# A recurrence's operands loaded in the fifth and sixth step of its chain, and a square placed between two transposes

## The chip, the cores and the metric

One NeuronCore of a Trainium2 chip. The time is that of one execution on the device, in microseconds; of several runs the median counts. Engines are called as in the profile: PE is TensorE, DVE VectorE, ACT ScalarE, POOL GpSimd, and SP is SyncE, which in this kernel only issues DMAs.

## The reference

Two layers of an encoder for 512 tokens of width 1024: layer 0 mixes tokens by windowed attention, layer 1 by a recurrence in both directions (RWKV-7), and a convolutional feed-forward part follows each. The change concerns the recurrence alone. Cut to what matters:

```python
def wkv7_scan(r, w, k, v, a, bb, reverse):          # per head, state 64 x 64
    def step(state, inp):
        r_t, w_t, k_t, v_t, a_t, b_t = inp
        sa = jnp.einsum('bhvk,bhk->bhv', state, a_t)
        state = state * w_t[:, :, None, :] + sa[..., None] * b_t[:, :, None, :] + v_t[..., None] * k_t[:, :, None, :]
        y = jnp.einsum('bhvk,bhk->bhv', state, r_t)
        return state, y
...
    y = y_f + y_b                                    # forward and backward scan, 16 heads
    mean = jnp.mean(y, axis=-1, keepdims=True)
    var = jnp.mean(jnp.square(y - mean), axis=-1, keepdims=True)
    yn = ((y - mean) * lax.rsqrt(var + RWKV_GN_EPS)).reshape(b, s, d) * lnx_w.astype(F32) + lnx_b.astype(F32)
    out = (yn + (bonus_f + bonus_b).reshape(b, s, d)) * g.astype(F32)
    return out.astype(h.dtype) @ w_o
```

## The kernel before

The 16 heads are handled as eight column tiles of two heads each (`ct`, 0 to 7); the 512 tokens of a tile are eight chunks of 64, in both directions `d`. For each tile the projections (`rwkv_proj`) make four scaled operands and store them to HBM: `ar` holds [a | r], `bk` holds [b | k], each 1 MB for a tile with both directions. `rwkv_scan` then works on a tile in stages:

- `prep` loads `bk` and `ar` of a tile. There are two buffers for `bk` and three for `ar`, so a load waits for the last reader of an older tile.
- `low` multiplies `ar` with `bk` on PE; DVE masks the products into `bw` (line 943). `blocks` stores the diagonal blocks to HBM (`ls`), `loaded` reads them back in another layout as `X`.
- `solve` inverts these triangular blocks in 31 small steps, three on POOL, seventeen on DVE, the rest on POOL (lines 1005 and 1007). DVE copies the result (line 913, `X<-Y`), `kept` stores it (`zs`), `inverses` reads it back as `t32` (`t` in the trace) and `tt`, and `level` makes the full inverses of it.
- `tokens` transposes `bk` on PE, ACT copies the result into `bw` (line 911). `sides` transposes `a` and multiplies with `v` (lines 981 and 983).
- `batch` combines all into the chain's matrices; `step` is one step of the chain: products with the state on PE, and the scaling to the next state on ACT (line 1124, `st`), in seven of the eight steps.
- `head_norm` normalizes a finished tile in five parts (`n0` to `n4`); part `n1` squares on ACT (line 1147), and the last stores the tile (`os`).

`run` goes through the tiles in iterations `i` from -1 to 7. An iteration walks through the eight strings of `K.between`, one per step; `c` is the chain's step for tile `i`, and the other letters are parts for the same or a later or earlier tile: `m1` and `n` finish tile `i` and tile `i - 1`, `t`, `a`, `L`, `x0`, `x1`, `m0`, `z`, `I` belong to tile `i + 1`, `l`, `b`, `X` and the solving steps `G`, `V` to tile `i + 2`, and `p` loads tile `i + 3`. `e` loads `gt` and `bo`, which `n4` needs.

All instructions from the start of `run` on are tied to the order in which they are written, engine by engine; the DMAs too, since SP issues them all. What is ahead of `run` (projections, `low` of tiles 0 and 1, the first inverse) is ordered by the compiler's scheduler.

Of the kernel before, what the change touches and what calls it, by code (L numbers as in the profile page):

```python
# [52 lines left out]
def paced(K, later, earlier):  # L53

    K.tc.add_manual_dep(later.ins, earlier.ins.name,
                        mybir.DependencyInfo(mybir.DependencyClass.Sync, mybir.DependencyReason.DATA), reason="pace")
# [766 lines left out]
def rwkv_scan(K, A, sc, mid):  # L823

    nc = K.nc
# [5 lines left out]
    R = Ctx()  # L831
# [22 lines left out]
    def mk(shape, name, bufs=1, dt=F32):  # L854
        pool = mid if name in MID else pools[next((k for k, v in PLACE.items() if name in v), "batch")]
        return pool.tile(shape, dt, name=name, tag=name, bufs=bufs)
# [17 lines left out]
    def spare(n):  # L874
        pool = R.pre.enter_context(tc.tile_pool(name=f"pre{len(R.pres)}", bufs=1, space=PSUM, side="right", reuse_waits="tile"))
        R.pres += [pool.tile([P, S], F32, name=f"pre{i}") for i in range(n)]
# [7 lines left out]
    def start():  # L884

        pools["early"] = first.enter_context(tc.tile_pool(name="early", bufs=1, side="right", reuse_waits="tile"))
        spare(K.npre)
        R.ARs, R.BKs, R.BWs = [], [], []
        inputs(1)
        R.Xs, R.nX = [mk([P, 32, 32], "X0")], 0  # L890
        R.cs = []
        R.done = dict.fromkeys("pls", 0)

    R.start = start

    def inputs(n, bks=True):

        for _ in range(n):
            R.ARs.append(mk([P, 2, 2, NC, HD], f"ar{len(R.ARs)}"))
            if bks:  # L900
                R.BKs.append(mk([P, 2, NC, 2, HD], f"bk{len(R.BKs)}"))
            R.BWs.append(mk([P, 2, NC, 2, 3 * HD], f"bw{len(R.BWs)}").rearrange("p d c e s -> p c d e s"))
# [16 lines left out]
    def prep(ct):  # L919

        c = Ctx()
        ar, bk = R.ARs[ct % len(R.ARs)], R.BKs[ct % len(R.BKs)]
        c.AR, c.BK = [ar[:, d] for d in range(2)], [bk[:, d] for d in range(2)]
        nc.sync.dma_start(out=bk, in_=sc["bk"][ct].rearrange("d p c z s -> p d c z s"))
        nc.sync.dma_start(out=ar, in_=sc["ar"][ct].rearrange("d p z c s -> p d z c s"))
        return c

    def bk(c, d, e, q):

# [2 lines left out]
    def low(ct, c, g):  # L932


        c.BW = R.BWs[ct % len(R.BWs)]
        hf, d = GROUPS[g]
        pvs = [bank().rearrange("p (c s) -> p c s", c=4) for _ in range(2)]
        for i in range(4):
            q = 4 * hf + i
            for e in range(2):  # L940
                T.matmul(pvs[e][:, i], lhsT=bk(c, d, e, q), rhs=c.AR[d][er(e), :, at(d, q)], start=True, stop=True)
        for e in range(2):
            V.tensor_tensor(out=c.BW[:, 4 * hf:4 * hf + 4, d, e, 0:P], in0=pvs[e],
                            in1=R.mask[:, d, None, :].broadcast_to([P, 4, P]), op=ALU.mult)

    def blocks(ct, c, d):

        for h in range(2):
            nc.sync.dma_start(out=sc["l"][ct, h, d].rearrange("c e i j -> i c e j"),
                              in_=c.BW[qr(d, h), :, d, :, 32 * h:32 * h + 32])  # L950

    def loaded(ct, c):
        c.X = block()
        for b in range(2):
            nc.sync.dma_start(out=c.X[er(b)], in_=sc["l"][ct].rearrange("h d c e i j -> (h d c e) i j"))
# [59 lines left out]
    def kept(ct, c):  # L1015
        zd = sc["z"][ct]
        for d in range(2):
            nc.sync.dma_start(out=zd[0, 48 * d:48 * d + 16], in_=c.Z[0][HD + 48 * d:HD + 48 * d + 16])
        nc.sync.dma_start(out=zd[1], in_=c.Z[1][0:HD])

    def go(ct, c, n, by):

        c.by = by
        if not hasattr(c, "solving"):
            c.solving = solve(ct, c)
        for _ in range(n):
            next(c.solving, None)
# [152 lines left out]
    def stages(names):  # L1180

        for x in names:
            ct = R.done[x]
            R.done[x] += 1
            K.ct = ct
            if x == "p":
                R.cs.append(prep(ct))
            elif x == "l":
                for g in range(4):
                    low(ct, R.cs[ct], g)  # L1190
                for d in range(2):
                    blocks(ct, R.cs[ct], d)
                loaded(ct, R.cs[ct])
            else:
                go(ct, R.cs[ct], 32, "G")
                kept(ct, R.cs[ct])
# [5 lines left out]
    def part(i, q):  # L1202

        x, args = q[0], [int(k) for k in q[1:].split(",") if k]
        if x == "p":
            while len(R.cs) <= min(i + 3, KT - 1):
                K.ct = len(R.cs)
                R.cs.append(prep(K.ct))
            return
        if x in "xm":  # L1210
            k, fn, args = i + (q != "m1"), batch, [args[0], int(x == "m")]
        else:
            k, fn = i + PARTS[x][0], PARTS[x][1]
            if x in "GVgv":
                fn, args = go, args + [x.upper()]
        if 0 <= k < KT and not (x == "z" and k == 0) and not (x in "lbX" and k < R.done["l"]):
            K.ct = k
            fn(k, R.cs[k], *args)

    def run(last):  # L1220
# [13 lines left out]
        for i in range(-1, KT):  # L1234
            more = None
            if i == KT - 1:
                first.close()
                more = last(R)
            for j in range(NC):
                K.ct = max(i, 0)  # L1240
                for q in K.between[j].split():
                    if q == "c":
                        K.ct = i
                        if i >= 0:
                            step(i, R.cs[i], j)
                    else:
                        part(i, q)
                if more and j:
                    next(more, None)
# [24 lines left out]
def body(ctx, tc, A, out, stage=9):  # L1274
    nc = tc.nc
    K = Ctx()
# [47 lines left out]
    K.begin, K.tail = (2,), ("pl", "", "", "")  # L1324
    K.ny = 2
    K.eng.update(z0="V", z1="V")
    K.between = ("w0 c l0 l1 b0 u g4", "c l2 l3 b1 g4 z X I", "c m1 w1 n0 e", "c n1 t0 t1 G3", "c a0 n2 V6", "c L0 n3 V6", "c L1 a1 n4 p V5", "c x0 x1 m0 G4")
    const = ctx.enter_context(tc.tile_pool(name="const", bufs=1, reuse_waits="tile"))

    @contextmanager  # L1330
# [54 lines left out]
    def ffn(layer, xT, st, nxt, nst, store):  # L1385
# [4 lines left out]
    sc = {"ar": dram.tile([KT, 2, P, 2, NC, HD], F32, name="ars"), "bk": dram.tile([KT, 2, P, NC, 2, HD], F32, name="bks"),  # L1390
          "v": dram.tile([S, D], F32, name="vs"), "g": dram.tile([KT, P, S], F32, name="gs"),
          "bo": dram.tile([KT, P, S], F32, name="bos"), "o": dram.tile([KT, P, S], F32, name="os"),
          "l": dram.tile([KT, 2, 2, NC, 2, 32, 32], F32, name="ls"), "z": dram.tile([KT, 2, HD, 32, 32], F32, name="zs")}
# [14 lines left out]
    if stage <= 1:  # L1408
        for e in (xstack, products, left, banks):
            e.close()  # L1410
        return
    scan = rwkv_scan(K, A, sc, mid)
    scan.late, scan.pre = left, banks
    rwkv_proj(K, xT, st, xstack, products, A, sc, scan)

    with ExitStack() as end:
# [64 lines left out]
        with tc.tile_pool(name="act2", bufs=1, reuse_waits="tile") as K.act:  # L1481
            K.accp = K.work = K.act
            on_tile = residual(xT, "nch1" if stage > 2 else None, st if stage > 2 else None, out if stage == 2 else None)
            for ot in range(KT):
                ps = scan.bank()
                c = slice(ot * P, (ot + 1) * P)
# [84 lines left out]
```

## Time and profile before

| | |
|---|---|
| runs | 1612.32, 1612.32, 1610.83 us; median 1612.32 |
| profiled execution | 1611.12 us, of which the span from first to last instruction is 1608.9 |
| PE busy | 1481.5 us (92%) |
| DVE, ACT, POOL busy | 1033.6 (64%), 689.9 (43%), 441.8 (27%) |
| chain that ended last, by engine | PE 67%, DVE 14%, DMA 7%, POOL 5%, issue 4% |
| loads of `ar`, of `bk` | 8 each, 1024 KB, median 8.5 and 5.2 us from issue to landing |

The busy shares are means over the whole program, and the stages differ: the feed-forward layers fill PE, the scan (about 929 to 1173 us of the span) does not. The chain that ended last is followed back from the last instruction; a DMA in it means that an engine waited for this transfer.

### The profile page before, as it was taken

What the parts mean: (1) busy time and instruction counts of PE and PEld (TensorE: products, weight loads), DVE (VectorE), ACT (ScalarE), POOL (GpSimd) and SP (SyncE); (2) the same over time, 40 slices, a digit from 0 to 9 for tenths busy, and PEclk for the clock granted to TensorE, in tenths of its full rate; (3) what the DMA queues carried; (4) which work ended last, traced back from release to release, by engine and by line L of the source; (5) the groups of instructions that cost most, each with busy time, mean ns of one, the idle gap of its engine ahead of it and who ended that gap; (6) DMA issues with size and microseconds to landing.
All of it is one profiled execution on the core that took longest, in us unless ns stands there. A gap on an engine that the chain in (4) does not pass through costs nothing.

```text
span 1608.9 us, 28508 instructions
## 1 busy us (share of the span) xinstructions
PE 1481.5 (92%) x11612; PEld 1198.3 (74%) x11612; DVE 1033.6 (64%) x1643; ACT 689.9 (43%) x1228; POOL 441.8 (27%) x533
## 2 busy tenths in 40 slices
PE   8989999999999998989987588777889999999999
PEld 7767688888888886767765477666767888888887
DVE  6876457777773348968988656665547677777222
ACT  5576534444432224556543343333444444444111
POOL 2630003222310015425488423223200333221000
PEclk9999999999999999999996597888899999999999
DMA  5200022333233332446536545555343222323331
GB/s 187 79 27 1 11 95 92 99 98 99 97 99 112 101 95 66 131 154 216 188 140 200 167 107 140 135 134 142 82 161 130 92 92 92 101 96 102 103 120 56
DMA packets 108834, 178.56 MB, mean 111 GB/s; under 512 B 49184, under 2 KB 62112, under 8 KB 108704
## 3 DMA queue, kind: packets, MB, share of 16 engines
q1 hardware_dynamic: 108560, 176.75, 36.2%
q8 instruction: 91, 1.49, 0.4%
q14 instruction: 39, 0.32, 0.1%
q10 hardware_dynamic: 144, 0.00, 0.0%
HBM read 142.64 MB, written 34.08 MB: 110 GB/s over the span
## 4 chain that ended last, share of the span: by engine, by line
PE 67%; DVE 14%; DMA 7%; POOL 5%; issue 4%; ACT 2%; SPq 1%; DVEq 0%; POOLq 0%; ACTq 0%
PE mm L113 17%; PE mm L111 16%; PE mm L112 16%; DMA ar<-ars 2%; PE mm L394 2%; PE sc L111 2%; PE sc L112 2%; PE sc L113 2%; DMA X<-ls 2%; POOL Y L1007 2%; PE tp L389 2%; DVE wlo L78 1%; POOL tg L1005 1%; DVE tv L1005 1%; DMA ls<-bw 1%
## 5 line engine op out<-in xcount | busy, mean ns | idle before, releaser
L75 ACT CAST whi<-wraw 128x1024 fp32r<-128x1024 f32 (+1 forms) x197 | 201.0, 1022 | 258.2 <-PE mm L112 179.4
L111 PE MATMUL mm<-hl,whi 128*128 128x512 f32 x720 | 281.3, 391 | 2.0 <-DVE xT L1368 1.8
L113 PE MATMUL mm<-hl,wlo 128*128 128x512 f32 x720 | 281.7, 391 | 0.8 <-POOL wlo L78 0.4
L112 PE MATMUL mm<-hl,whi 128*128 128x512 f32 x720 | 281.0, 390 | 0.0
L78 DVE TENSOR_TENSOR wlo<-wraw,whi 128x1024 fp32r<-128x1024 f32 (+1 forms) x140 | 167.1, 1194 | 170.2 <-ACT whi L75 169.7
L78 POOL TENSOR_TENSOR wlo<-wraw,whi 128x1024 fp32r<-128x1024 f32 x57 | 136.7, 2398 | 400.6 <-ACT whi L75 386.8
L192 DVE SCALAR_TENSOR_TENSOR conv<-upad,par,conv 128x512 f32<-128x512 f32 x88 | 125.6, 1429 | 64.1 <-ACT conv L189 64.1
L113 PEld LDWEIGHTS mm<-hl,wlo 128*128 128x128 f32 x720 | 135.6, 188 | 32.4 <-POOL wlo L78 3.1
L111 PEld LDWEIGHTS mm<-hl,whi 128*128 128x128 f32 x720 | 135.5, 188 | 30.2 <-ACT hl L98 2.2
L112 PEld LDWEIGHTS mm<-hl,whi 128*128 128x128 f32 x720 | 135.6, 188 | 28.3
L113 PE MATMUL mm<-gh,wlo 128*128 128x512 f32 x352 | 139.0, 395 | 0.0
L111 PE MATMUL mm<-gh,whi 128*128 128x512 f32 x352 | 139.0, 395 | 0.0
L112 PE MATMUL mm<-gl,whi 128*128 128x512 f32 x352 | 139.0, 395 | 0.0
L104 ACT CAST gh<-gact 128x512 fp32r<-128x512 f32 x44 | 27.4, 623 | 140.4 <-DVE gact L201 140.4
L189 ACT ACTIVATE conv<-upad,par 128x512 f32<-128x512 f32 x88 | 71.7, 816 | 21.7 <-DVE upad L187 21.5
L113 PEld LDWEIGHTS mm<-gh,wlo 128*128 128x128 f32 x352 | 66.1, 188 | 16.1
L111 PEld LDWEIGHTS mm<-gh,whi 128*128 128x128 f32 x352 | 66.1, 188 | 16.1
L112 PEld LDWEIGHTS mm<-gl,whi 128*128 128x128 f32 x352 | 66.1, 188 | 16.0
L1005 POOL TENSOR_TENSOR tg<-X,Y 128x56 f32<-128x56 f32 (+16 forms) x129 | 46.3, 359 | 111.3 <-DVE Y L1007 81.3
L194 DVE SCALAR_TENSOR_TENSOR conv<-upad,par,conv 128x512 f32<-128x512 f32 x88 | 70.1, 798 | 3.0
L1124 ACT ACTIVATE st<-bank,gc 128x64 f32<-128x64 f32 x112 | 29.5, 318 | 91.4 <-PE bank L1121 87.5
L199 ACT ACTIVATE silu<-conv 128x512 f32<-128x512 f32 x44 | 27.9, 634 | 91.2 <-DVE conv L194 91.2
(334 smaller groups left out, 3148.4 us busy)
## 6 DMA issues: line engine op xcount, KB each, us to landing
wraw<-in_w_up_dram SPq DMA_DIRECT2D x88, 512.0 KB, 3.6
wraw<-in_w_down_dram SPq DMA_DIRECT2D x32, 512.0 KB, 3.6
ars<-tab SPq DMA_DIRECT2D x16, 512.0 KB, 2.7
bks<-tab SPq DMA_DIRECT2D x16, 512.0 KB, 3.4
ar<-ars SPq DMA_DIRECT2D x8, 1024.0 KB, 8.5
bk<-bks SPq DMA_DIRECT2D x8, 1024.0 KB, 5.2
wraw<-in_w_down_dram SPq DMA_DIRECT2D x16, 384.0 KB, 3.2
wraw<-in_w_qkv_dram SPq DMA_DIRECT2D x11, 512.0 KB, 4.3
```

The lines of the kernel that those rows point to most:

```text
L75: nc.scalar.copy(out=hi, in_=raw)
L78: lo_engine.tensor_tensor(out=lo, in0=raw, in1=hi.bitcast(F32), op=ALU.subtract)
L111: nc.tensor.matmul(ps, lhsT=lhs[0], rhs=rhs[0], start=first, stop=False)
L112: nc.tensor.matmul(ps, lhsT=lhs[0], rhs=rhs[1], start=False, stop=False)
L113: nc.tensor.matmul(ps, lhsT=lhs[1], rhs=rhs[0], start=False, stop=last)
L189: nc.scalar.activation(out=c, in_=u[:, 1:S + 1], func=AF.Identity, scale=K.par[:, cw + 2 * FT + ch:cw + 2 * FT + ch + 1], bias=K.par[:, cb ...
L192: nc.vector.scalar_tensor_tensor(out=c, in0=u[:, 0:S], scalar=K.par[:, cw + ch:cw + ch + 1], in1=c, op0=ALU.mult, op1=ALU.add)
L194: nc.vector.scalar_tensor_tensor(out=c, in0=u[:, 2:S + 2], scalar=K.par[:, cw + 4 * FT + ch:cw + 4 * FT + ch + 1], in1=c, op0=ALU.mult, op ...
L389: nc.tensor.transpose(out=tp[:, j * P:(j + 1) * P], in_=p[:, e, j * P:(j + 1) * P], identity=K.ident)
L394: nc.tensor.matmul(po[e * HD:(e + 1) * HD, n], lhsT=vn[:, n - 1 + j, kv * HD:(kv + 1) * HD], rhs=pT[:, e, j * P:(j + 1) * P], start=n == 0 ...
L1005: en.tensor_tensor(out=tm, in0=X[:, 0:kx, kx:kx + 1].broadcast_to([P, kx, n]), in1=Y[:, kx:kx + 1, m:16].broadcast_to([P, kx, n]), op=ALU. ...
L1007: en.tensor_tensor(out=Y[:, 0:kx, m:16], in0=Y[:, 0:kx, m:16], in1=tm, op=ALU.add)
```

## The change

`prep` becomes a generator. It loads each direction of `bk` and of `ar` by a DMA of its own, 512 KB each, first `bk`, then `ar`. Once the chain runs (`R.pace` is then the last scaling on ACT), each load waits for that scaling, and `prep` stops after `bk`; the new letter `q` lets it go on with `ar`. `p` moves from the seventh string of `K.between` (behind `n4`) to the fifth, `q` stands in the sixth, and in the fourth `n1` moves from ahead of both transposes to between them.

```diff
         R.done = dict.fromkeys("pls", 0)
+        R.pace = R.prep = None
...
-        nc.sync.dma_start(out=bk, in_=sc["bk"][ct].rearrange("d p c z s -> p d c z s"))
-        nc.sync.dma_start(out=ar, in_=sc["ar"][ct].rearrange("d p z c s -> p d z c s"))
-        return c
+        for x, name in ((bk, "bk"), (ar, "ar")):
+            for d in range(2):
+                src = sc[name][ct, d]
+                ld = nc.sync.dma_start(out=x[:, d], in_=src)
+                if R.pace:
+                    paced(K, ld, R.pace)
+            if R.pace:
+                yield c
+        yield c
...
             if x == "p":
-                R.cs.append(prep(ct))
+                R.cs.append(next(prep(ct)))
...
         if x == "p":
             while len(R.cs) <= min(i + 3, KT - 1):
                 K.ct = len(R.cs)
-                R.cs.append(prep(K.ct))
+                R.prep = prep(K.ct)
+                R.cs.append(next(R.prep))
+            return
+        if x == "q":
+            if R.prep:
+                next(R.prep, None)
+                R.prep = None
             return
...
-    K.between = ("w0 c l0 l1 b0 u g4", "c l2 l3 b1 g4 z X I", "c m1 w1 n0 e", "c n1 t0 t1 G3", "c a0 n2 V6", "c L0 n3 V6", "c L1 a1 n4 p V5", "c x0 x1 m0 G4")
+    K.between = ("w0 c l0 l1 b0 u g4", "c l2 l3 b1 g4 z X I", "c m1 w1 n0 e", "c t0 n1 t1 G3", "c a0 p n2 V6", "c L0 q n3 V6", "c L1 a1 n4 V5", "c x0 x1 m0 G4")
```

On SP, the end of the third string to the start of the next iteration, before (`gt`, `bo`: operands of the last part of the norm; `os`: the store of a normalized tile; `ls`: the blocks for the next inverse):

```order
L1037 DMA tt0_7306<-zs_78 32x16x32 x4
L1062 DMA gt_8592<-gs_74 128x512
L1064 DMA bo_8594<-bos_75 128x512
L1166 DMA os_76<-t_8902 128x512
L924 DMA bk0_5951<-bks_72 128x2x1024
L925 DMA ar1_7303<-ars_71 128x2x1024
L949 DMA ls_77<-bw1_7305 32x16x32 x2
```

The loads of a later tile stand behind the store here. The same place on SP now:

```order
L1044 DMA tt0_7308<-zs_78 32x16x32 x4
L1069 DMA gt_8600<-gs_74 128x512
L1071 DMA bo_8602<-bos_75 128x512
L928 DMA bk0_5951<-bks_72 128x1024 x2
L928 DMA ar1_7305<-ars_71 128x1024 x2
L1173 DMA os_76<-t_8914 128x512
L956 DMA ls_77<-bw1_7307 32x16x32 x2
```

The loads have changed places with the store, and are four instead of two. In the first iteration of the chain there is no `gt`, `bo` or `os`, and the loads stand behind `tt` in both.

On ACT, the fourth step, before (`st`: the scaling; `t_8612`: the square; `bw`: the copies of the transposes, two for each direction):

```order
L1124 ACTIVATE st_8600<-bank_8546,gc_5023 128x64 x2
L1147 ACTIVATE t_8612<-t_8590 128x512
L911 COPY bw2_7483<-mm_7301 128x8x64
L911 COPY bw2_7483<-mm_7302 128x8x64
L911 COPY bw2_7483<-pre0_5948 128x8x64
L911 COPY bw2_7483<-pre1_5949 128x8x64
L1124 ACTIVATE st_8671<-bank_8607,gc_5023 128x64 x2
```

Here the square stands ahead of all four copies. The same step on ACT now:

```order
L1131 ACTIVATE st_8608<-bank_8554,gc_5023 128x64 x2
L912 COPY bw2_7487<-mm_7303 128x8x64
L912 COPY bw2_7487<-mm_7304 128x8x64
L1154 ACTIVATE t_8638<-t_8598 128x512
L912 COPY bw2_7487<-pre0_5948 128x8x64
L912 COPY bw2_7487<-pre1_5949 128x8x64
L1131 ACTIVATE st_8679<-bank_8615,gc_5023 128x64 x2
```

The square has moved behind the first direction's two copies; nothing else differs in this step.

On SP in the projections, where the scheduler places the first tile's loads (`ar_5950`, `bk_5951`) among the stores of a later tile's operands (`tab`), before and now:

```order
-L775 DMA ars<-tab 128x1024
-L779 DMA bks<-tab 128x1024
-L925 DMA ar_5950<-ars 128x2x1024
-L61 DMA wraw<-in_wk_dram 128x1024
-L924 DMA bk_5951<-bks 128x2x1024
...
+L928 DMA ar_5950<-ars 128x1024
+L775 DMA ars<-tab 128x1024
+L928 DMA bk_5951<-bks 128x1024
+L779 DMA bks<-tab 128x1024
```

The first half of each load has moved ahead of the stores; in what follows, `low` of tile 0 and the first solving steps stand a few instructions earlier on PE, DVE and POOL, and before the end of the projections one half of tile 2's `bk` stands on SP ahead of the last tile's loads and stores.

## Rows read from the trace of the kernel before

**Rows 1.** Busy time in two stretches: PE, PEld, DVE, ACT, POOL, granted clock, DMA.

```profile
1020.00:1080.00 60.00, 45.78 (x1089) 40.76 (x1089) 37.13 (x97) 20.66 (x60) 18.46 (x54) 0.83 0.48 127
...
972.00:984.00 12.00, 10.09 (x274) 9.10 (x274) 5.97 (x19) 5.38 (x14) 4.01 (x10) 0.57 0.64 146
```

**Rows 2.** Timeline of DVE, the copies of finished inverses: start, duration, [idle before].

```profile
935.62 2.10 DVE L913 COPY X<-Y 64x512 f32<-64x512 f32 x4
...
967.84 2.09 DVE L913 COPY X<-Y 64x512 f32<-64x512 f32 x4 [0.45 <-POOL Y L1007]
...
1004.03 2.08 DVE L913 COPY X<-Y 64x512 f32<-64x512 f32 x4
...
1079.99 2.09 DVE L913 COPY X<-Y 64x512 f32<-64x512 f32 x4
...
1118.34 2.09 DVE L913 COPY X<-Y 64x512 f32<-64x512 f32 x4
...
1150.65 2.07 DVE L913 COPY X<-Y 64x512 f32<-64x512 f32 x4 [6.90 <-POOL Y L1007]
```

**Rows 3.** Timeline of ACT, first and second scalings of some iterations.

```profile
960.89 0.52 ACT L1124 ACTIVATE st<-bank,gc 128x64 f32<-128x64 f32 x2 [0.49 <-PE bank L1110]
963.48 0.52 ACT L1124 ACTIVATE st<-bank,gc 128x64 f32<-128x64 f32 x2 [2.07 <-PE bank L1121]
...
995.55 0.52 ACT L1124 ACTIVATE st<-bank,gc 128x64 f32<-128x64 f32 x2 [0.49 <-PE bank L1110]
...
1031.39 0.52 ACT L1124 ACTIVATE st<-bank,gc 128x64 f32<-128x64 f32 x2 [0.49 <-PE bank L1110]
...
1066.16 0.52 ACT L1124 ACTIVATE st<-bank,gc 128x64 f32<-128x64 f32 x2 [0.49 <-PE bank L1110]
1076.02 0.52 ACT L1124 ACTIVATE st<-bank,gc 128x64 f32<-128x64 f32 x2 [9.34 <-PE bank L1121]
...
1104.86 0.52 ACT L1124 ACTIVATE st<-bank,gc 128x64 f32<-128x64 f32 x2 [0.49 <-PE bank L1110]
```

**Rows 4.** Timeline of PE, the first products of `low` after 1066 us.

```profile
1071.51 2.08 PE L941 MATMUL mm<-ar,bk 64*128 64x128 f32 x16 [5.23 <-DMA ar<-ars]
```

**Rows 5.** Timeline of SP's queue: issue, time that the issue took.

```profile
946.44 0.38 SPq L924 DMA_DIRECT2D bk<-bks  x1
...
1062.07 0.32 SPq L1166 DMA_DIRECT2D os<-t  x1
...
1062.92 0.50 SPq L925 DMA_DIRECT2D ar<-ars  x1
...
1090.31 0.43 SPq L1064 DMA_DIRECT2D bo<-bos  x1
1100.66 0.32 SPq L1166 DMA_DIRECT2D os<-t  x1
```

**Rows 6.** DMA issues of the page: count, KB each, us from issue to landing.

```profile
wraw<-in_w_up_dram SPq DMA_DIRECT2D x88, 512.0 KB, 3.6
```

**Rows 7.** Timeline of DVE, the last masked products of the iteration of 960.89.

```profile
966.11 1.28 DVE L943 TENSOR_TENSOR bw<-mm,mask 128x512 f32<-128x512 f32 x2
```

**Rows 8.** Timelines of ACT and PE (square, `sides`); then tile `t`, 1080 to 1100 us.

```profile
1085.09 0.63 ACT L1147 ACTIVATE t<-t 128x512 f32<-128x512 f32 x1 [2.84 <-DVE t L1144]
...
1086.25 0.48 PE L981 MATMUL pre<-ident,ar 64*64 64x64 f32 x4 [1.17 <-ACT bw L911]
...
L1047 PE MATMUL mm<-t,bw x64: 236/236/258, 1091.2 to 1092.1; 32*32 32x32 f32 x64
...
L1034 SPq DMA_DIRECT2D t<-zs x2: 486/502/519, 1086.3 to 1086.9; - x2
...
DMA to landing us min/median/max: 3.7/3.8/3.8
```

**Rows 9.** Timelines of POOL and DVE in the projections: the first solving step, a late operand.

```profile
803.95 0.45 POOL L1005 TENSOR_TENSOR tg<-X,Y 128x31 f32<-128x31 f32 x1 [2.75 <-DMA X<-ls]
...
900.00 1.60 DVE L773 TENSOR_TENSOR tab<-tr,ts 128x512 f32<-128x512 f32 x1 [1.42 <-DMA ars<-tab]
```

## The prediction

> **What bounds the kernel now.** I read the busy time by stretch first, then the waits and the timeline of the scan. In the feed-forward layers the TensorE matmuls fill the time; from 929 to 1173 us, where the eight column tiles go through the recurrence, no engine does. In the stretch 1020 to 1080 TensorE is busy 45.78 of 60 us and VectorE 37.13 [rows 1], so chains of waits set the pace there. Nothing of the change touches the work elsewhere, so the sum is made for this stretch, with one term for the stretch ahead of it.
>
> Each iteration of the scan runs the eight-step chain of one tile, the triangular inverse of the next tile and the products `low` of the tile after that. I take as its mark the moment when VectorE starts to copy a finished inverse (line 913, `X<-Y`). These marks stand at 935.62, 967.84, 1004.03, one left out, 1079.99, 1118.34 and 1150.65 [rows 2]: distances of 32.2 us, 36.2, twice 38.0 on average, 38.4, and 32.3. The second and the last mark show that VectorE was waiting for GpSimd's last solving step, so two distances of about 32.3 us are what the inverse itself takes to come round: load, solve, store. The four distances between, 967.84 to 1118.34, are 150.5 us together, 21.3 more than four times 32.3.
>
> What makes these four long is one wait. In the iteration that begins at 1066.16 the chain's second scaling comes 9.86 us after the first; in the iteration of 960.89 it is 2.59 us [rows 3]. Between them TensorE stands 5.23 us until `ar` has landed, and then runs at half speed (16 products in 2.08 us) [rows 4]. The load is late because it is issued late: SyncE's queue gives out the store `os` at 1062.07 and the load of `ar` at 1062.92 [rows 5], and it lands when TensorE has long been waiting. That store waits for the normalized output of the previous tile, a VectorE operation in the seventh step. In the next iteration the queue's last work before `os` is the load of `bo` at 1090.31; `os` follows at 1100.66, ten microseconds of empty queue later. The iteration of 929 shows what happens without that store: there the loads go out from 946.44 on [rows 5], 10.8 us after the mark of 935.62, `low` doesn't wait for it, and the distance is 32.2 us.
>
> **The loads.** Each iteration issues four half loads where it issued two whole ones, and it issues them ahead of `os`. Their place on the queue is behind `bo`, so in the iteration of 1066.16 they begin at 1090.75 instead of behind 1100.66: 10.8 us after the mark. The two holds (the fifth and sixth scaling) stand in front of nothing on the path: in this iteration the fifth scaling is over before `bo` is issued, the sixth comes at about the time when `bk` has gone out, and behind the held loads stands only `os`, which nobody reads before the end of the scan. The halves carry the same bytes. `ar` whole took from 1062.92 to 1071.51, 8.6 us; the nearest half-megabyte load takes 3.6 us [rows 6]. Side by side or one after the other (8.6 to 14.4 us), the four halves have landed 19 to 25 us after the mark. They are wanted when the next iteration starts: 27.7 us after the mark at 995.55, 27.4 at 1031.39, 24.9 at 1104.86 [rows 2, 3]. I take the lower end, because the iteration of 929 issues its loads at the same point.
>
> The wait for `ar` then goes, and two things can be late next. One is the inverse: 32.3 us. The other is the chain: mark to next first scaling, and from there to the last masked product, which has to be through VectorE before the next mark. That tail is 966.11 + 1.28 - 960.89 = 6.5 us in an iteration without stall [rows 3, 7]. So the chain gives 27.7 + 6.5 = 34.2 us, 33.9 and 31.4 for the first, second and fourth of the four distances (the third is like the fourth). The larger of chain and inverse counts: 34.2 + 33.9 + 32.3 + 32.3 = 132.7, **a gain of 17.8 us**. Its upper bound is 21.3, all four at 32.3.
>
> **The square.** On ScalarE the norm's square now stands behind the first two copies of the transposes instead of ahead of all four. It ran at 1085.09 after a wait for VectorE, the copies came behind it, and TensorE's next batch, `sides`, began at 1086.25, after 1.17 us of waiting for the first of them [rows 8]. The transposes that feed those two copies were done well before, so the copies fit into the wait and `sides` begins up to 1.17 us earlier. The square itself isn't later: its input ends at the same time. How much of it reaches the next scaling depends on the small load `t` behind `sides`: issued 1086.3 to 1086.9, landing 3.8 us later, at 1090.1 to 1090.7, while the products that read it start at 1091.2 [rows 8]. So 0.5 to 0.6 us is free in that iteration. I take 0.6 each for the two distances that the chain sets (the other two are set by the inverse), which makes them 33.6 and 33.3, **a gain of 1.2 us**, and 0.5 for the last iterations; bounds 0 and 1.2 in each.
>
> **Two terms against it.** The loads now run beside the small loads of the inverse and beside `gt` and `bo`, in a stretch that had none of them. Nothing of the trace prices that in the late iterations; the iteration of 929 has it and keeps 32.2 us (below: 0), and 1 us in each of four (above: 4) would be twice the 0.5 us for which `t` lay ready. I take 1.0, nearer to the iteration that has it.
> The scheduler also reorders the end of the projections, because the first tile's loads come in halves: `low` of tile 0 moves up, GpSimd meets the first solving step before the small subtractions `tlora`, and a half load of `bk` stands ahead of the last tile's loads and stores on SyncE. GpSimd stood 2.75 us for that first X, which is the most this could give back; VectorE stood 1.42 us for a store of `ars` [rows 9], and a half load in front adds at most its 3.6: 5.0 against. I take 1.0 against.
>
> **Sum.** 17.8 + 1.2 + 0.5 - 1.0 - 1.0 = 17.5 us. The profiled execution took 1611.1 us (span 1608.9 and 2.2 around it), so it would take 1593.6. The median shown is 1612.3, 1.2 above the profiled one, hence **1594.8 us**. The bounds: gain at least 17.8 - 4 - 5.0 = 8.8, time 1603.5; at most 21.3 + 1.2 x 2 + 2.75 = 26.5, time 1585.9.
>
> **Rivals.**
> *The clock gives more.* [...] Chance 0.15.
> [...]
>
> *A new wait takes half back.* The halves land late after all, or push the small loads of the inverse (`t`, `tt`, X) back by 2 to 3 us, and all four distances settle near 35: 150.5 - 140 = 10 us less the other terms, about 1603. For it: the window before `t` lands is only 0.5 us wide. Against it: the iteration of 929. Chance 0.13.
>
> *No change.* The loads wait for something else than their place: each holds the tile's old reader and the holds. The last reader of `bk` is the pair of transposes of the fourth step, of `ar` the sums of the third; both are over when `bo` goes out. Chance 0.06, 1612.
>
> *Slower.* GpSimd, in order, now stands at the first solving step of tile 0 with `tlora` behind it, and `tlora` feeds the next tile's products. If the first X comes later than the scheduler thought, every projection tile behind it is put off. It decides once that costs more than the 17.5 us plus 3.2, 20.7 in all, over the last tiles: 7.5 times the 2.75 us that GpSimd stood there. Time then 1616 or more. Chance 0.06.
>
> **How the numbers follow.** The forecast, 1590 to 1600 by itself, has 0.60. Something like 0.2% (3.2 us) is what a measurement of this kernel can tell from no change. The range 1587 to 1604 takes in the forecast, the clock and most of the case of half back, and leaves out no change and slower. Faster: 0.60 + 0.15 + 0.13 = 0.88; same 0.06; slower 0.06.
>
> **What the changed profile would show.** Right: `ar` halves issued about 11 us after the mark, ahead of `os`; no wait of TensorE for `ar`; first to second scaling under 3 us in every iteration; marks 32 to 34 us apart; `sides` without its wait for the copies. Wrong: marks still near 36 to 38 with TensorE waiting for `t`, `tt` or the masks; `ar` still named as what ends a wait; or a first scaling of the first chain later than 929 by more than 5 us, which would put the loss into the projections.

## The result, and the profile after

The changed kernel takes 1593.2 us (median of four, 1592.4 to 1597.0), the kernel before beside it 1611.6 (median of four): a ratio of 0.9897, 95% interval 0.9877 to 0.9916. The profiled execution of the changed kernel is the slowest of its four, 1597.0 us with a span of 1594.9; against the profiled one of before, the span is 14.0 us shorter.

The marks come first: the timeline of DVE in the changed kernel, the copies of finished inverses (line 914 now).

```profile
934.12 2.09 DVE L914 COPY X<-Y 64x512 f32<-64x512 f32 x4
967.50 2.08 DVE L914 COPY X<-Y 64x512 f32<-64x512 f32 x4
...
1068.91 2.08 DVE L914 COPY X<-Y 64x512 f32<-64x512 f32 x4 [0.79 <-POOL Y L1014]
1102.67 2.09 DVE L914 COPY X<-Y 64x512 f32<-64x512 f32 x4
1135.50 2.07 DVE L914 COPY X<-Y 64x512 f32<-64x512 f32 x4 [5.91 <-POOL Y L1014]
```

Set beside [rows 2], the four distances from 967.50 to 1102.67 are 135.2 us together, where they were 150.5: 15.3 us won. The first distance has grown from 32.2 to 33.4, the last from 32.3 to 32.8. The first mark stands 1.5 us sooner; behind the last mark the span is 1.2 us longer. That is 15.3 - 1.2 - 0.5 + 1.5 - 1.2 = 13.9, the difference of the spans but for rounding.

That `ar` no longer stands in the way is read from ACT's first and second scaling of one iteration, and from SP's queue (issue, time that the issue took) in the iteration of the mark 1068.91.

```profile
1061.62 0.52 ACT L1131 ACTIVATE st<-bank,gc 128x64 f32<-128x64 f32 x2 [0.49 <-PE bank L1117]
1064.21 0.52 ACT L1131 ACTIVATE st<-bank,gc 128x64 f32<-128x64 f32 x2 [2.07 <-PE bank L1128]
```

```profile
1080.16 0.43 SPq L1071 DMA_DIRECT2D bo<-bos  x1
1080.70 0.85 SPq L928 DMA_DIRECT2D bk<-bks  x2
1081.65 0.96 SPq L928 DMA_DIRECT2D ar<-ars  x2
1089.47 0.32 SPq L1173 DMA_DIRECT2D os<-t  x1
```

From the first scaling to the second it is 2.59 us, in every iteration that still runs `low` (before 9.86 in this place, [rows 3]). The halves go out 11.8 to 13.2 us after the mark, ahead of `os`, and no wait of TensorE names `ar` any more; before, four of its waits did, 15.0 us in all (1.88, 2.50, 5.23 and 5.42). What TensorE waits for instead stands in its timeline of the same iteration.

```profile
1073.91 0.27 PE L988 MATMUL pre<-ident,ar 64*64 64x64 f32 x2
...
1079.10 0.32 PE L1054 MATMUL mm<-t,bw 32*32 32x32 f32 x4 [2.19 <-DMA t<-zs]
1080.51 1.07 PE L1054 MATMUL mm<-t,bw 32*32 32x32 f32 x60 [1.10 <-DMA t<-zs]
...
1089.07 0.37 PE L1133 MATMUL bank<-st,qt 64*64 64x64 f32 x2 [1.85 <-issue]
```

`sides` (line 988) begins 5.0 us after the mark instead of 6.3, without its wait for the copies, as foretold. But then TensorE stands 3.3 us for `t`, and the products that read `t` end 12.7 us after the mark; before, the last of them began at 1092.1 [rows 8], 12.1 after its mark, and took 0.2. Some 6 us on comes a wait that is marked "issue": TensorE waits for nothing that a semaphore shows. The groups of TensorE's waits between the first and the last mark (us in total, times, longest) sum it up.

```profile
PE mm L1054 <- DMA t<-zs: 9.6, 6, 3.2
PE pre L1054 <- DMA t<-zs: 7.5, 4, 2.8
PE pre L1057 <- issue: 2.4, 2, 2.0
...
PE bank L1133 <- issue: 1.8, 1, 1.8
...
PE pre L990 <- issue: 1.4, 1, 1.4
PE mm L1083 <- issue: 1.4, 1, 1.4
...
PE mm L988 <- issue: 1.1, 1, 1.1
```

So 17.1 us go to `t` over six distances, and 8 to "issue"; before it was 4.2 and 6.2. The granted clock follows: in the table by stretch (columns as in [rows 1]), the 7 us that hold the wait for `t` and the 12 us behind them.

```profile
1073.91:1080.91 7.00, 3.72 (x124) 3.36 (x124) 1.73 (x5) 3.41 (x9) 3.99 (x10) 0.84 0.98 157
1080.91:1092.91 12.00, 10.14 (x298) 9.52 (x290) 10.54 (x36) 4.77 (x14) 0.18 (x1) 0.66 0.64 241
```

In these 12 us the granted clock is 0.50 from 1080.91 to 1085.5 and from 1089.0 to 1092.3, and 1.00 in between and behind: two thirds of the stretch at half speed. What half speed is in time shows in the kernel before: the 16 products of [rows 4] took 2.08 us at a granted clock of 0.50, 16 of the same shape 1.16 us at 1.00 (from 960.94 and from 1076.28 on). The kernel before, in the same two stretches behind its mark of 1079.99:

```profile
1084.99:1091.99 7.00, 5.82 (x148) 5.31 (x148) 1.63 (x5) 4.49 (x11) 4.00 (x10) 0.59 1.09 188
1091.99:1103.99 12.00, 10.43 (x327) 9.29 (x318) 10.87 (x37) 7.07 (x20) 0.07 (x1) 0.81 0.31 92
```

So half speed is nothing new here: it stood ahead of the products that read `t` (0.59, and 0.81 behind them), and now it stands behind them (0.84, then 0.66). The chain from mark to next first scaling is 26.2 to 27.5 us in the four middle iterations, all near the long values of before (27.7 and 27.4), none near the short ones (24.2 and 24.9).

### The profile page after: what moved, and what is told of

It reads as the page before. It is cut to its first block, busy times and chain, and to the rows that moved or that the text cites. A ratio compares the mean times of both kernels' runs of the same rounds, so it can differ in the third digit from the quotient of the medians.

```text
span 1594.9 us, 28561 instructions
## 1 busy us (share of the span) xinstructions
PE 1482.9 (93%) x11612; PEld 1199.9 (75%) x11612; DVE 1032.0 (65%) x1643; ACT 688.6 (43%) x1228; POOL 440.6 (28%) x533
## 4 chain that ended last, share of the span: by engine, by line
PE 73%; DVE 12%; DMA 4%; issue 4%; POOL 3%; ACT 3%; SPq 1%; DVEq 0%; POOLq 0%; ACTq 0%
PE mm L113 17%; PE mm L111 17%; PE mm L112 17%; PE mm L394 2%; PE sc L111 2%; PE sc L112 2%; PE sc L113 2%; PE tp L389 2%; DVE wlo L78 1%; DMA t<-zs 1%; PE sc L374 1%; DVE bw L950 1%; DVE sf L537 1%; DMA ls<-bw 1%; DMA ars<-tab 1%
## 5 line engine op out<-in xcount | busy, mean ns | idle before, releaser
L78 DVE TENSOR_TENSOR wlo<-wraw,whi 128x1024 fp32r<-128x1024 f32 (+1 forms) x140 | 170.9, 1222 | 169.3 <-ACT whi L75 168.9
L189 ACT ACTIVATE conv<-upad,par 128x512 f32<-128x512 f32 x88 | 71.5, 815 | 17.9 <-DVE upad L187 17.7
L113 PE MATMUL mm<-sx,wlo 128*128 128x512 f32 (+1 forms) x144 | 59.9, 416 | 5.4 <-DVE wlo L78 5.4
```

The lines of the kernel that those rows point to most:

```text
L78: lo_engine.tensor_tensor(out=lo, in0=raw, in1=hi.bitcast(F32), op=ALU.subtract)
L113: nc.tensor.matmul(ps, lhsT=lhs[1], rhs=rhs[0], start=False, stop=last)
L189: nc.scalar.activation(out=c, in_=u[:, 1:S + 1], func=AF.Identity, scale=K.par[:, cw + 2 * FT + ch:cw + 2 * FT + ch + 1], bias=K.par[:, cb ...
```

## The experiments

**Theories.** A: `t` holds the chain. It lands when it did, TensorE reaches it too early, stands, and runs at half speed behind it. B, the rival: the big loads hold the chain. They now run while TensorE needs its next piece of code and the last small loads. Below, "the six distances" is the time from the first to the seventh mark: 215.0 us before, 201.4 in the changed kernel's profile.

**The changed kernel again** (control, no edit).

> The changed kernel once more, unchanged, as the measure for the others of this group. Both theories: 1592 to 1597 us; first scaling of the first chain at 927.5 (within 0.5 if the 1.5 us won ahead of the scan belong to the program, nearer to 929 if they were chance); marks 33.4 to 34.0 us apart.

Measured: 1594.64 us (1590.87 to 1596.65), ratio 0.9896, interval 0.9879 to 0.9914. First scaling at 927.48, as expected; the distances lie between 32.2 and 35.6 us, wider than the 33.4 to 34.0 that were expected, and the six come to 204.6, 3.2 us more than the profile before it with the same order. So a single profile of this kernel tells the distances to a few us only.

**The square back** in front of the transposes, the loads at the new place.

```diff
-    "c t0 n1 t1 G3"
+    "c n1 t0 t1 G3"
```

> The loads at their new place, the square back ahead of both transposes. Theory A (the small load t holds the chain: TensorE now reaches the first product that reads t too early, waits 1.2 to 2.8 us and runs at half speed behind that): sides begins 1.25 us later after the mark, the wait for t shrinks by as much, the marks stay 33.5 to 34 us apart, time within 1 us of the control. The prediction's own term for the square: 1.2 + 0.5 = 1.7 us slower than the control, marks 0.3 to 0.6 us further apart in the distances that the chain sets.

Measured: 1596.83 us, 0.9907 (0.9887 to 0.9926), six distances 201.6. `sides` starts 6.2 to 6.3 us after six of the seven marks, and the wait for `t` falls from 17 to 19 us to 7.6. That is 2.2 us over the control, more than either expectation, but the intervals overlap; the distances are those of the changed kernel.

**The square alone**, the loads as before.

```diff
-    "c n1 t0 t1 G3"
+    "c t0 n1 t1 G3"
```

> The kernel before with the square between the transposes, the loads where they were. Sides begins 1.25 us sooner after the mark. Theory A: TensorE waits for t instead, and the wait for ar behind it stays 5 us; within 1.5 us of the kernel before, distances between the marks as there (215 us in all, 212 to 217). The prediction's term: 1.2 to 1.7 us faster than the kernel before.

Measured: 1612.64 us, 1.0001 (0.9991 to 1.0011), so nothing is won; the six distances are 220.1, outside what was expected. The groups of TensorE's waits between the first and the last mark:

```profile
PE pre L941 <- DMA ar<-ars: 11.8, 2, 6.5
PE mm L941 <- DMA ar<-ars: 8.7, 2, 6.3
PE pre L1047 <- DMA t<-zs: 8.0, 6, 3.1
PE mm L1047 <- DMA t<-zs: 7.8, 5, 3.8
```

The wait for `t` has risen from 4.2 us to 15.8: what the square gives, that wait takes.

**No loads in the chain.**

```diff
+        old = ct if ct < 3 else 2 - ct % 2
-        ar, bk = R.ARs[ct % len(R.ARs)], R.BKs[ct % len(R.BKs)]
+        ar, bk = R.ARs[old % len(R.ARs)], R.BKs[old % len(R.BKs)]
...
+                if ct > 2:
+                    continue
...
```

> No loads of ar and bk in the chain: tiles 3 to 7 work on the operands and decays of tiles 1 and 2 again, all else as in the changed kernel. Theory B: the waits of TensorE for its code (1.1 to 2.0 us in each iteration) and the half speed behind them go, marks 32.3 to 32.6 apart, 5 to 7 us faster than the control. Theory A: the wait for t stays at 2 to 3 us an iteration, marks 33 to 34 apart, under 2 us faster than the control.

Measured: 1587.48 us, 0.9859 (0.9836 to 0.9882), 7.2 us under the control. Its marks in the timeline of DVE, and the same two stretches of the fifth iteration:

```profile
1062.48 2.10 DVE L914 COPY X<-Y 64x512 f32<-64x512 f32 x4 [2.10 <-POOL Y L1017]
1094.64 2.10 DVE L914 COPY X<-Y 64x512 f32<-64x512 f32 x4 [2.11 <-POOL Y L1017]
```

```profile
1067.48:1074.48 7.00, 7.00 (x174) 6.58 (x176) 2.23 (x7) 3.87 (x10) 3.98 (x10) 0.50 1.14 205
1074.48:1086.48 12.00, 10.72 (x328) 9.51 (x326) 10.94 (x37) 7.56 (x22) 0.66 (x2) 0.90 0.09 29
```

DVE waits for GpSimd's last solving step at every mark but the first: the inverse sets all distances, 32.1 us in four and 32.9 in two, 194.3 in all. Against 201.4 and 204.6 the loads cost 7 to 10 us over six distances. This is B's size. But the waits marked "issue" don't go: 5.6 us stay, where the changed kernel has 8, in places where they stood with the loads too.

**The second `sides` early**, as work for the time in which TensorE waited for `t`.

```diff
-    "c L0 q n3 V6", "c L1 a1 n4 V5"
+    "c a1 L0 q n3 V6", "c L1 n4 V5"
```

> The second sides (a1) ahead of the product that reads t instead of behind the one that reads tt: 2.9 us of TensorE work in the place where it waited. Theory A: the wait for t is gone or under 0.5 us, fewer stretches at half speed, chain from mark to first scaling 25 to 26 us instead of 26.2 to 27.5, so that the inverse (32.3) sets most distances: 1 to 1.5 us in each of five, 5 to 7 us faster than the control. Theory B (the big loads, now beside TensorE's code loads and tt, hold the chain; the wait for t is only cover for them): waits for code and half speed stay, distances 33.3 to 34, within 1.5 us of the control.

Measured: 1591.14 us, 0.9876 (0.9855 to 0.9897), six distances 199.9. TensorE's largest waits between the first and the last mark, but for those on DVE:

```profile
PE mm L1057 <- issue: 3.8, 1, 3.8
PE pre L1054 <- DMA t<-zs: 3.8, 3, 2.2
PE pre L1057 <- issue: 3.2, 2, 1.7
PE pre L1083 <- issue: 3.2, 2, 2.4
```

The wait for `t` is down to 3.8 us, and the waits marked "issue" are up to 12.9. The distances stay near 200 in all (32.1 to 34.7 each); the first mark comes 2.9 us sooner (931.2). The time is 3.5 us under the control's, between A's 5 to 7 and B's 1.5, with intervals that overlap: this run alone decides for neither.

**Filling the wait** with products that nobody reads, to see what becomes of the clock and of the time.

```diff
-        q = bank()[:, 0:256].rearrange("p (c s) -> p c s", s=32)
+        full = bank()
+        if k == 0:
+            for _ in range(10):
+                T.matmul(full[:, 384:512], lhsT=K.ident, rhs=K.ident, start=True, stop=True)
+        q = full[:, 0:256].rearrange("p (c s) -> p c s", s=32)
```

> The changed kernel with ten products of the identity with itself in front of the first product that reads t, into a part of its bank that nobody reads: some 2 to 2.5 us of TensorE work in each iteration, in the place where it waited for t. t lands when it did. If the half speed behind the wait is what lengthens the chain: the clock stays at or near full until the next wait, the six distances between the marks fall from 201.4 to 204.6 us to 194 to 199, 3 to 7 us faster than the control. If the loads and the code do it by themselves: distances 200 to 205, time within 2 us of the control or slower by up to 3 where the filling overhangs.

Measured: 1595.93 us, 0.9899 (0.9885 to 0.9913), six distances 200.3. The two stretches of the fifth iteration, then TensorE's waits between the first and the last mark:

```profile
1073.57:1080.57 7.00, 7.00 (x206) 6.65 (x206) 1.79 (x5) 3.79 (x10) 3.99 (x10) 1.00 0.96 179
1080.57:1092.57 12.00, 7.83 (x252) 6.83 (x252) 10.48 (x36) 6.13 (x18) 0.24 (x1) 0.87 0.67 226
```

```profile
PE mm L990 <- issue: 4.4, 1, 4.4
PE mm L1087 <- issue: 3.6, 1, 3.6
...
PE pre L988 <- issue: 3.0, 1, 3.0
...
PE pre L990 <- issue: 1.7, 1, 1.7
```

The clock is up (0.87 instead of 0.66 here, 1.00 in two other iterations, 0.92 instead of 0.84 over the six distances), `t` is waited for 2 us in all, and nothing is won: TensorE, faster now, stands 13.7 us at "issue". The half of theory A that blames the half speed falls here: on this evidence TensorE would have waited in that time anyhow. The other half, that the chain has to wait for `t`, isn't tested here, since `t` lands when it did; the second `sides` early took 13 us of that wait away and left the distances near 200.

**The halves held by the seventh scaling**; the order of every engine and queue is the same.

```diff
-    "c a0 p n2 V6", "c L0 q n3 V6", "c L1 a1 n4 V5"
+    "c a0 n2 V6", "c L0 n3 V6", "c L1 a1 p q n4 V5"
```

> The order of every engine and queue as in the changed kernel, but the four halves wait for the seventh scaling instead of the fifth and sixth, so they begin 13 to 15 us after the mark instead of 11 to 12, and have landed after 21 to 24. Theory B, by the place of the loads: TensorE's half speed and waits for code shift or shrink, and the distances change by more than 0.5 us each, to either side. Theory A (wait for t alone): nothing changes, sum of the six distances 200 to 205 us, time within 1.5 us of the control.

Measured: 1591.34 us (1591.12 to 1592.83), 0.9876 (0.9861 to 0.9891); six distances 197.7. Now "issue" shows something. In the changed kernel TensorE stands at it in each of the first five iterations (1.35, 2.00, 1.40, 1.07, 1.85 us), each time at another place of the program. Of these five only the second is left here, 2.37 us, and that one stands in the kernel without loads too (2.25); the sixth iteration, 0.38 us in the changed kernel, has 2.25 here. What comes in these waits is seen in the DMA queues in half a microsecond, first of the changed kernel in 1086.50 to 1087.00, then of this one in 1080.50 to 1081.00.

```profile
DMA packets 52, 0.19 MB, mean 385 GB/s; under 512 B 8, under 2 KB 8, under 8 KB 51
## 3 DMA queue, kind: packets, MB, share of 16 engines
q1 hardware_dynamic: 51, 0.18, 90.5%
q8 instruction: 1, 0.02, 12.2%
```

```profile
DMA packets 1, 0.02 MB, mean 33 GB/s; under 512 B 0, under 2 KB 0, under 8 KB 0
## 3 DMA queue, kind: packets, MB, share of 16 engines
q8 instruction: 1, 0.02, 11.7%
```

In both there is one packet of 0.02 MB on a queue that the profile calls "instruction". That such packets are TensorE's code, and that "issue" is a wait for them, is read from the counts. The page of the changed kernel has 91 of them:

```profile
q8 instruction: 91, 1.49, 0.4%
```

That is 16,384 bytes each, and TensorE has 23,341 instructions in this trace: 256 to a packet. In all 14 profiles together TensorE stands at "issue" for over 0.2 us 73 times between the first and the last mark. Each time it stops at the same place (within one) in its row of 256 instructions, and goes on 2.2 to 3.6 us behind the start of a packet.

The third packet of the iteration comes 17.7 us after the mark in the changed kernel, beside 51 packets of the queue of loads and stores, and 1.85 us of waiting end 2.4 us behind it. Held to the seventh scaling, the halves go out 14.1 us after the mark, and the packet comes at the same 14.1, with nothing else in that half microsecond. In two other iterations it is 17.1 against 14.7, and 15.2 against 14.4; in a third, where 1.40 us of waiting went, it is 14.3 against 14.0 to 14.5, and TensorE came later to that place.

A packet could also be late because TensorE itself comes late to that part of its code. So I count from the moment when TensorE came to the place before, 256 instructions ahead. For the packets of the five waits that is 3.85, 2.49, 2.68, 2.86 and 2.79 us in the changed kernel, 0.95, 2.44, 2.02, 1.06 and 0.48 with the halves held, and 0.79, 2.25, 1.68, 1.32 and 0.75 without loads. Over all 14 profiles the median is 0.4 us for the 150 packets that had less than 0.05 MB of other transfers in the 2 us ahead of them, and 3.0 us for the 72 that had over 0.6 MB. Holding the halves doesn't take the delay away; it moves it to the next packet, which comes 3.0 to 4.0 us behind in the five iterations. This one is that of the fifth, in 1086.50 to 1087.00:

```profile
q1 hardware_dynamic: 50, 0.20, 100.1%
q8 instruction: 1, 0.02, 12.8%
```

Behind it TensorE stands for under 0.3 us; that the instructions ahead of that place take it longer is the author's estimate. Of the 35 packets between the first and the last mark of the changed kernel six make TensorE stand for over 0.3 us; the six cost 8 us, and the waits of the filled kernel 13.7.

**Both: the second `sides` early and the halves held by the seventh scaling.**

```diff
-    "c a0 p n2 V6", "c L0 q n3 V6", "c L1 a1 n4 V5"
+    "c a0 n2 V6", "c a1 L0 n3 V6", "c L1 p q n4 V5"
```

> The second sides ahead of the product that reads t, as in the kernel that does that alone, and the four halves held by the seventh scaling. If both the wait for t and the loads' place count: 2 to 4 us faster than the former, 1587 to 1589 us. If only one of them does: the same as the former, 1591 us, sum of the six distances about 200.

Measured: 1587.17 us (1585.16 to 1589.66), 0.9849 (0.9832 to 0.9866): 4 us under each of the two by the medians, with intervals that still touch theirs, while its interval lies below the control's. Three of its marks on DVE, and two stretches of the fifth iteration:

```profile
1028.71 2.09 DVE L914 COPY X<-Y 64x512 f32<-64x512 f32 x4 [2.10 <-POOL Y L1014]
1060.87 2.09 DVE L914 COPY X<-Y 64x512 f32<-64x512 f32 x4 [2.06 <-POOL Y L1014]
1093.02 2.10 DVE L914 COPY X<-Y 64x512 f32<-64x512 f32 x4 [2.10 <-POOL Y L1014]
```

```profile
1065.87:1072.87 7.00, 6.91 (x208) 6.58 (x207) 2.23 (x7) 4.26 (x11) 3.99 (x10) 0.76 1.09 179
1072.87:1084.87 12.00, 9.71 (x288) 7.92 (x290) 10.94 (x37) 7.15 (x22) 0.66 (x2) 1.00 0.61 220
```

The loads are there (DMA share 0.61), and still the inverse sets every distance: 193.7 us for the six, as without loads. The wait for `t` is 1.3 us; that for code is 6.3, in nine pieces of at most 1.3, where the changed kernel has 8. So the sum of these waits by itself isn't what was won. Of the time won 2.6 us lie ahead of the first mark (931.48).

**The same with the square back** (its one edit is that of the kernel with the square back).

> The fastest so far (second sides ahead of the product that reads t, halves held by the seventh scaling) with the square back ahead of both transposes. If the inverse sets all distances there, the square is worth nothing: within 1.5 us of it (1586 to 1589 us), distances 193.5 to 195 in all. If the chain is near to setting them again: first products 1.2 us later, one or two distances over 32.6, 1 to 3 us slower.

Measured: 1588.49 us, 0.9852 (0.9838 to 0.9866), six distances 194.6: the square is worth nothing here either.

**No holds**: the four halves wait for no scaling.

```diff
-                if R.pace:
-                    paced(K, ld, R.pace)
```

> The changed kernel without the holds of the four halves, so they go out as soon as SyncE has given out bo. The fifth scaling comes 6.6 us after the mark, the sixth 8.0, the first half 10.8 to 12.9: the holds are over by then. Both theories: no difference, 1592 to 1597 us, distances 200 to 205 in all, first half issued 11 to 13 us after the mark.

Measured: 1594.01 us, 0.9887 (0.9873 to 0.9901), as expected; the first half goes out 9.9 to 11.9 us after the mark. The six distances are 197.8, lower than expected: with the same order, three profiles gave 197.8, 201.4 and 204.6. So the 197.7 of the halves held by the seventh scaling prove nothing by themselves; what stands is how late each packet of code came. Without holds, too, four of the five waits are there (1.72, 2.53, 1.46 and 2.40 us).

**Whole loads ahead of the scan, and whole loads everywhere.**

```diff
+        if not R.pace:
+            nc.sync.dma_start(out=bk, in_=sc["bk"][ct].rearrange("d p c z s -> p d c z s"))
+            nc.sync.dma_start(out=ar, in_=sc["ar"][ct].rearrange("d p z c s -> p d z c s"))
+            yield c
+            return
```

> As the changed kernel, but what is loaded ahead of the scan (tiles 0 to 2) is loaded whole, as before the change, so the projections keep their old order; in the chain the halves stay. If the halves are what won 1.5 us ahead of the scan: first scaling at 929.0 instead of 927.5, time 1.5 us over the control, marks 33.4 to 35 apart as there. The prediction's own term had the other sign: 1 us faster than the control.

Measured: 1594.73 us, 0.989 (0.9872 to 0.9909). The first scaling comes at 926.93, no later than with halves (927.48 and 927.53), so the halves ahead of the scan are worth nothing measurable either way.

And for whole loads everywhere:

```diff
-            for d in range(2):
...
+        for x, name, how in ((bk, "bk", "d p c z s -> p d c z s"), (ar, "ar", "d p z c s -> p d z c s")):
+            ld = nc.sync.dma_start(out=x, in_=sc[name][ct].rearrange(how))
             if R.pace:
+                paced(K, ld, R.pace)
                 yield c
```

> Two whole loads of 1 MB, in the new places and with the holds, instead of four halves. Theory B (the big loads at this point of an iteration hold the chain) with the bytes as the cause: the same as the kernel with whole loads ahead of the scan alone, within 1 us, sum of the six distances between the marks 200 to 205 us. If the number of transfers counts: fewer waits of TensorE for code, distances 0.5 to 1 us shorter, 3 to 6 us faster.

Measured: 1592.66 us, 0.9891 (0.9872 to 0.9909), six distances 199.6 against 202.2 with halves in the chain: within the scatter. No effect of the size of the transfers can be seen.

## Why the prediction was right

1593.6 was forecast for the profiled execution and 1594.8 for the median; measured were 1597.0 and 1593.2. The main step held. The profiled execution won 13.9 us by its parts, where 17.5 were forecast: the four distances 15.3 instead of 18.0 (17.8 + 1.2 - 1.0), the first and last distance -1.7 instead of 0, what lies behind the last mark -1.2 instead of 0.5, and what lies ahead of the first +1.5 instead of -1.0. So the median came this near with some luck: the terms that were wrong have different signs.

- **The loads, 17.8 us.** Right in its mechanism: issued 10.8 to 13.2 us after the mark, ahead of `os`; no wait for `ar`; second scaling 2.59 us behind the first. The size: with the square's 1.2 the four distances were to come to 131.5 us. They were 135.2 in this profile, 138.6 in the control, 132.4 without holds. The prediction took the third and fourth to be set by the inverse, because the chain of these two had been 24 to 25 us long. In the changed kernel the chain of all four takes 26.2 to 27.5, and only at one mark (1068.91, 0.79 us) does DVE still wait for GpSimd.
- **The loads beside other transfers, 1.0 us.** This is the term that was mis-sized. Without the loads the four distances are 129.3; with them, in the same order of work, 132.4 to 138.6. That is 3.1 to 9.3 us, against bounds of 0 and 4 (3.5 to 10 us over six distances). The prediction looked at the small loads and at `gt` and `bo`, and took the iteration of 929 as its witness; it did not think of TensorE's code, which comes by DMA too, and later where these loads run (3.0 us instead of 0.4 by the medians above). Even that witness waits for code in the changed kernel, 1.35 us.
- **The square, 1.7 us.** Wrong: worth nothing by itself (1612.64 us, 1.0001, 0.9991 to 1.0011). The step that failed took the landing of `t` in one iteration, 0.5 us ahead of its readers, for all of them, and let the square's gain reach the next scaling. The sign foretold for this came true: TensorE waits for `t`.
- **The reordering ahead of the scan, -1.0 us.** Nothing that can be measured: with the old order the first scaling comes at 926.9, with the new one at 927.5. The two kernels that load as before in the chain too have 929.0 and 928.3; what makes that difference stays open.
- **The rivals.** The clock gave less where TensorE had waited for `t`, not more: 0.66 in the 12 us from 1080.91 on, 0.81 in the same stretch of the kernel before. In the kernel without loads the inverse sets all four distances, 129.3 us (four times 32.3 is 129.2), with a clock of 0.89 over the six instead of 0.84. But the filled kernel has 0.92 and keeps its long distances (200.3 us in all), so a higher clock by itself isn't what shortens them here. "A new wait takes half back" named `t` and came true in part: its four distances were to be 140 us, 8.5 above the forecast, and this profile has 3.7 of them. "No change" and the slower case are out.
- **The bounds.** The upper bound adds 2.4 us for the square to the 21.3 of four distances all set by the inverse; in that case the square can give nothing, and the bound is 2.4 us too wide.

The profiled execution is the slowest of four, 3.8 us above their median; in which stretch these lie stays open, as an execution without a profile shows no stretches.

**What stays open.** That code comes later where the loads run is shown by the packets; how the DMA engines order the two isn't. How this delay becomes 7 to 10 us of distance is in part argued: between the changed kernel and the one without loads the waits for code differ by 2.4 us only, the waits for `t` by 9.5 (17.1 and 7.6), and the clock is 0.84 and 0.89; which of these follow from the late code no run separates. How the last 7 us divide between the second `sides` and the later hold isn't settled: alone the two give 1591.1 and 1591.3 us, each within reach of the control's runs, and only together they lie clear of it.

## What to carry to other kernels

A load that is issued earlier leaves its old wait but meets other traffic: list what else comes by DMA at the new place. Here TensorE's own code did, 2.5 to 3.9 us behind TensorE in front of the five waits. A stall that disappears from an engine's front is only worth what the next late thing behind it leaves; filling the stall, which raised the mean clock behind it from 0.66 to 0.87, told here which one that was (13.7 us at "issue"). Once the order of a queue is right, the hold can still be moved: a transfer that can't avoid the other traffic can be put where what it delays isn't wanted so soon. Here this paid only together with a second move (1587.17 us, against 1591.34 and 1591.14 for each alone and 1594.64 for neither).

## What the runs showed of the hardware

TensorE's code came in packets of 16,384 bytes on a DMA queue of its own, 91 packets for 23,341 instructions in the changed kernel, one for 256 of them, five to six in an iteration (35 in six distances). Over the 14 profiles such a packet started 0.4 us (median of 150) after TensorE had come to the place 256 instructions ahead where under 0.05 MB of other transfers had been moved in the 2 us before, and 3.0 us after it (median of 72) where it was over 0.6 MB. Where it came too late, TensorE stood, 1.1 to 2.0 us in five iterations of the changed kernel and up to 4.4 in the filled one, under the label "issue"; shorter waits, and two of 4.1 us together, stood in the kernel without loads too. With TensorE kept busy through its wait for a load (7.00 of 7 us instead of 3.72), the granted clock of the 12 us behind was 0.87 instead of 0.66, and the time was the same: 1595.93 us, against 1594.64 for the control.
